# One step later for three pieces of side work, sixteen loads on another queue, and the last stores on two queues

## The chip, the cores and the metric

One NeuronCore of a Trainium2 chip runs the whole program in one launch. Its engines run side by side, each with its own instruction stream: TensorE (PE: matmuls and transposes), VectorE (DVE: elementwise work), ScalarE (ACT: copies and functions), GpSimd (POOL) and SyncE (SP: only issues DMAs). DMAs can be issued from SP, ACT and POOL; a DMA stands in the issuing engine's stream and waits there for what it needs. The metric is the device time of the program in microseconds (us), the median of the runs.

## The reference, cut to what matters

An encoder layer over x of 1024 rows and 2048 columns, in float32. `c` (one row of 2048) gives a shift, a scale and a gate for every column; the projections, the two branches and the output are large matmuls.

```python
mod = jax.nn.silu(c) @ w_ada + b_ada
shift, scale, gate = jnp.split(mod, 3, axis=-1)
h = rmsnorm(x, pre_g) * (1.0 + scale[:, None]) + shift[:, None]
q, k, v, gate_a, u, gate_p = jnp.split(h @ w_in, SPLIT_POINTS, axis=-1)
y_a = windowed_gqa(q, k, v, rel_table, sink) * jax.nn.silu(gate_a)
y_p = multiscale_pool(u, w_pool_grp, pool_scale) * jax.nn.silu(gate_p)
g_a, g_p = jnp.split(jax.nn.sigmoid(h @ w_merge + b_merge), N_BRANCHES, axis=-1)
merged = g_a * (y_a @ w_br_attn) + g_p * (y_p @ w_br_pool)
return x + gate[:, None] * rmsnorm(merged @ w_out, post_g)
```

## The kernel before

**Matmuls.** A float32 operand is split into a high and a low part that PE can multiply fast (`split`: ACT copies the high part, L96, DVE subtracts it to get the low part, L97), and a product is three matmuls: high by high, low by high, high by low. Over these lies a Strassen-like scheme (`strassen`): a block of the result comes from seven products instead of eight, named after their left operand, in the order B11, T3, T2, B21, T4, T1, B22. One product is 12 matmuls of 128x512 (6 in the first stage), into one of the PSUM banks X, V and Z. DVE and ACT add and copy the banks into one another (L114, L117, L257, L285, L302, L320); the copy of a bank is what frees it for a later product. Two of these generators overlap, so that the last product of one block (B22) runs after the first two of the next. The weights (`raw`, 512 KB a load) come from HBM through four buffers, are added to one another by DVE for the T products, and are split as above.

**Side work.** All that isn't a product hangs on these products. `run` goes through the seven, and after those that `every` lists it takes one step from a queue `side`:

```python
            if side and i in every:
                side.popleft()()
```

So a step's place in the list sets the place of its matmuls in PE's stream, and roughly that of its loads, ACT and DVE instructions. A scheduler then sets the order on every engine from program order and dependences; what is wrapped in `keep` stays in program order. Every engine works strictly through its order.

**The stages, and the side work that matters here.**

The ramp (to about 110 us) turns x, forms the columns of shift and scale for eight groups j of 256 columns and runs the first products. `late_sums` lists for its 13 side steps which parts of groups 2 and 3 they carry. A group's last part (`columns`) transposes the partial sums `acc` on PE into PM (L480), reduces them on DVE (L482) and adds and multiplies them into `modc` (L487, L490); the tiles xT are then scaled by `modc` on ACT (L567) and DVE (L568).

The first pass goes over 20 pairs of blocks of the left half of the inputs. Its side work sums further parts of w_ada into `gacc` (L536), and its last step `gate_row` takes the sums over rows with eight matmuls GATE (L885), adds and multiplies them on DVE and stores the gate's row to HBM (pg_d, L893); `late_rows` has eight matmuls PMR on the same line.

The rest of the first pass (from about 530 us) brings the right half of x. `x_step(n)` for n = 0 to 17 loads tile n (`fetch_x`, L958, load at L961, tag xt2), scales it on ACT (L962), and on every odd n transposes the tiles n-3 and n-2 on PE (`turn_x`, L968) and copies the pieces to h on ACT (L971).

The second pass has as side work the attention, the pooling, and at its end `y_steps`, which loads the 16 tiles of y_a back from HBM (ya_d, L1245) for the branch matmuls; four `pre` steps then subtract tiles y from one another on DVE (L117, tags y and tf). The same function loads y_p (yp_d) later.

At the end `out_pair` forms the output block by block. For the last two row tiles (t = 0, 1) `result` multiplies by the gate, `square` sums the squares on ACT (L1403), `scale_of` makes the row scale (L1420, L1421), and `finish_block` (L1424) multiplies by it, adds x (L1426) and stores 128x512 (L1427), for n in (0, 2, 3, 1). The block t = 1, n = 1 is the very last.

Of the kernel before, what the change touches and what calls it, by code (L numbers as in the profile page):

```python
# [15 lines left out]
AF = mybir.ActivationFunctionType  # L16
ALU = mybir.AluOpType
# [13 lines left out]
NB = S // P  # L31
# [12 lines left out]
def encoder_layer(ctx: ExitStack, tc: tile.TileContext, x, c, table, w_ada, b_ada, pre_g,  # L44
# [15 lines left out]
    nc = tc.nc  # L60
# [16 lines left out]
    def uid(s):  # L77
        cnt[0] += 1
        return f"{s}_{cnt[0]}"
# [11 lines left out]
    def keep(ins):  # L91

        tc.keep_in_program_order(ins)
# [25 lines left out]
    load = nc.sync.dma_start  # L119
    store = nc.sync.dma_start  # L120
# [9 lines left out]
    rstd = const.tile([P, NB], F32, name="rstd")  # L130
# [9 lines left out]
    ya_d = dram.tile([NH * P, S], F32, name="ya_d")  # L140
# [16 lines left out]
    def pre_op(j, h1, h2, tmp, pin=lambda ins: None):  # L157

        pin(sub(h1[j][1], h1[j][1], h1[j][0]))
        t2 = tmp()  # L160
        pin(sub(t2, h2[j][1], h1[j][1]))
        return t2
# [198 lines left out]
    held = ExitStack()  # L361
# [4 lines left out]
    for r0, src in ((0, c[0]), (16, b_ada[0, 0:D]), (32, b_ada[0, D:2 * D]),  # L366
                    (48, pre_g[0]), (64, b_merge[0]), (96, pool_scale[0])):
        n = src.shape[0] // P
# [133 lines left out]
    def modulation(j, tile_of, pin=False, apart=False):  # L502

        st_ = {}

        def step(q, between=None):
            if q == 0:
                st_["pv"] = bank("at", "GEMV")
            pv = st_["pv"]
            for kc in range(4 * q, 4 * q + 4):  # L510
                g = kc % 4 * 32
                ins = nc.tensor.matmul(pv[g:g + 32, :], scz[:, kc, :], tile_of(kc), start=kc < 4,
                                       stop=kc >= 12, tile_position=(0, g))
                if pin:
                    tc.keep_in_program_order(ins)
            if q == 3:
                acc = xa2.tile([P, 4, P], F32, tag="acc", name=uid("acc"), bufs=2)
                tc.keep_in_program_order(
                    nc.scalar.activation(acc, pv.rearrange("p (g n) -> p g n", g=4), AF.Copy))
                if between:  # L520
                    between()
                st_["acc"] = acc
                if not apart:
                    columns()

        def columns():
            mod_columns(j, sum_columns(st_["acc"]))

        return [partial(step, q) for q in range(4)] + [columns]
# [134 lines left out]

    group2 = modulation(2, ada[2].__getitem__, True, True)
    group3 = modulation(3, ada3.__getitem__, True, True)
    late_sums = {0: group2[:1], 4: group2[1:4], 5: group2[4:], 10: group3[:4], 11: group3[4:]}
    side = deque((lambda n=n: [step() for step in late_sums.get(n, ())]) for n in range(13))
    for s in range(2):
        for si in range(4 * s, 4 * s + 4):  # L670
# [249 lines left out]
    def unit_step(n):  # L920
        m = n - AHEAD
        if m in then:
            then[m]()
        if m >= 0:
            units[m][1]()
        if n < len(units):
            units[n][0]()

    side = deque(lambda n=n: unit_step(n) for n in range(len(units) + AHEAD))
    side.append(gate_row)  # L930
    EASY = ((0, 2, 4, 6), (1, 3, 5))
    n1 = 20
    sums = deque(weight_sums(j, h_) for h_ in range(2) for j in range(KT // 2))
# [24 lines left out]
    def fetch_x(si, q):  # L958
        xt = xin.tile([P, 512], F32, tag="xt2", name=uid("xt"))
        c0 = 1024 + q * 512  # L960
        load(xt, x[si * P:(si + 1) * P, c0:c0 + 512])  # L961
        nc.scalar.activation(xt, xt, AF.Copy, scale=rstd[:, si:si + 1])  # L962
        return xt

    def turn_x(si, q, xt):
        pt = bank("sc")
        for j in range(4):
            nc.tensor.transpose(pt[:, j * P:(j + 1) * P], xt[:, j * P:(j + 1) * P], ident)  # L968
        for j in range(4):
            dst = h[8 + q * 4 + j][si // 4][:, (si % 4) * P:(si % 4 + 1) * P]  # L970
            nc.scalar.activation(dst, pt[:, j * P:(j + 1) * P], AF.Copy)  # L971

    held = {}

    def x_step(n):
        if n < 2 * NB:
            held[n] = fetch_x(n // 2, n % 2)
        if n >= 3 and n % 2:
            for q in range(2):
                turn_x((n - 3) // 2, q, held.pop(n - 3 + q))  # L980

    side = deque(lambda n=n: x_step(n) for n in range(2 * NB + 2))
# [17 lines left out]
    side = deque()  # L1000
# [12 lines left out]
    with pool("attn") as ap:  # L1013
# [116 lines left out]
        def step(u, e):  # L1130
            nu = len(UNITS)
            if e == 0 and 0 <= u - LAG_V < nu:
                values(u - LAG_V)
            if e == 1 and u % 16 in (1, 3) and u < nu:
                turn_v(u % 16 // 2)
            if e == 1 and 0 <= u - LAG_T < nu:
                turn(u - LAG_T, 0)
                turn(u - LAG_T, 1)
            if u < nu:
                if u % 16 == 0 and e == 0:  # L1140
                    take_k(UNITS[u][0] * 2 // GQA)
                if u % 4 == 0:
                    split_q(e)
                scores(u, e)
            if e == 1:
                if opened:
                    gated(*opened.pop())
                if u % 4 == 3 and u + 1 < nu:
                    fetch_q(u + 1)
                c_ = u - LAG_V + 1  # L1150
                if (c_ + 1) % 16 == 0 and c_ + 1 < nu:
                    fetch_v(UNITS[c_ + 1][0] * 2 // GQA)
                if 0 <= c_ < nu:
                    if c_ % 4 == 0:
                        fetch_gate(c_)
# [83 lines left out]
    ysrc = ExitStack()  # L1239
    sp = ysrc.enter_context(pool("ysrc"))  # L1240

    def y_steps(yd, store_to):
        def get(k, s):
            t = sp.tile([P, 512], F32, tag="y", name=uid("y"), bufs=16)
            load(t, yd[k * P:(k + 1) * P, s * 512:(s + 1) * 512])  # L1245
            h1, h2, _ = store_to
            (h1 if k < 4 else h2).setdefault(k % 4, []).append(t)

        def pre(j):
            h1, h2, t2 = store_to  # L1250
            t2[j] = pre_op(j, h1, h2, lambda: sp.tile([P, 512], F32, tag="tf", name=uid("tf"), bufs=4), keep)

        return [lambda k=k, s=s: get(k, s) for k in (0, 4, 1, 5, 2, 6, 3, 7) for s in range(2)] + \
            [lambda j=j: pre(j) for j in range(4)]

    ys = [({}, {}, {}), ({}, {}, {})]
    side.extend(y_steps(ya_d, ys[0]))
    while side:
        next_pair(range(7))
    while pidx[0] < PAIRS:  # L1260
# [129 lines left out]
    def out_mm(pb, op, name, j, t, w, first, last):  # L1390
        ts_ = slice(t * P, (t + 1) * P)
        hi, lo = (o_[:, j % 2, ts_] for o_ in op[name][j // 2])
        nc.tensor.matmul(pb, hi, w[0], start=first, stop=False, skip_group_check=True)  # L1393
        nc.tensor.matmul(pb, lo, w[0], start=False, stop=False, skip_group_check=True)  # L1394
        nc.tensor.matmul(pb, hi, w[1], start=False, stop=last, skip_group_check=True)  # L1395

    xrow, held = {}, {}

    def rows_of(T, n):
        return out[T * P:(T + 1) * P, n * 512:(n + 1) * 512]  # L1400
# [18 lines left out]
    def scale_of(T, s_):  # L1419
        nc.scalar.activation(s_[:, 1:2], ssq[:, T, 1:2], AF.Sqrt, bias=s_[:, 0:1], scale=1.0 / D)  # L1420
        nc.vector.reciprocal(s_[:, 2:3], s_[:, 1:2])  # L1421
        return s_[:, 2:3]

    def finish_block(T, n, scale, store=store):  # L1424
        r = held.pop((T, n))
        keep(nc.vector.scalar_tensor_tensor(r, r, scale, xrow.pop((T, n)), op0=ALU.mult, op1=ALU.add))  # L1426
        store(rows_of(T, n), r)  # L1427

    def fetch_x_block(T, n, tile_of):
        xrow[T, n] = tile_of("xr")  # L1430
# [17 lines left out]
    def out_pair(half, i, op, between, after=None):  # L1448
# [51 lines left out]
        def result(blk, t, src, dst):  # L1500

            T, nh = half * 4 + (int(blk[1]) - 1) * 2 + t, int(blk[0]) - 1
            n = 2 * nh + i
            square(src, T, n)
            nc.vector.tensor_tensor(dst, src, g[nh], ALU.mult)
            if stays:
                held[T, n] = dst
            else:
                nc.gpsimd.dma_start(o_d[T * P:(T + 1) * P, n * 512:(n + 1) * 512], dst)
# [37 lines left out]
        for t in range(2):  # L1547
            for j, w in enumerate(last_weights):
                out_mm(bz[t], op, "B22", j, t, w, False, j == len(last_weights) - 1)
            result("12", t, bz[t], c12[t])  # L1550
            scale = scale_of(6 + t, rest[t])
            for n in (0, 2, 3, 1):
                finish_block(6 + t, n, scale)

    nextm, nextt2 = [], {}
    scales = {}
    side = deque()
# [79 lines left out]
    def third_block():  # L1637
        assert not side
        for T in (4, 5):
            scale = row_scale(T)  # L1640
            for b in range(4):
                finish_block(T, b, scale)

    out_pair(0, 0, ops[0], between_00)
    out_pair(0, 1, ops[0], between_01)
    out_pair(1, 0, ops[1], between_10)
    out_pair(1, 1, ops[1], between_11, third_block)

# [37 lines left out]
```

## Time and profile before

| what | before |
|---|---|
| runs | 2106.34, 2106.81, 2109.77 us; median 2106.81 |
| the profiled execution | 2109.9 us; its span 2107.8 us |
| PE busy | 2076.6 us (99%), 9511 matmuls |
| DVE, ACT, POOL busy | 1539.0 (73%), 1106.5 (52%), 25.5 us (1%) |
| chain that ended last | PE 90%, DMA 5%, DVE 3%, ACT 1% |
| DMA | 468.18 MB, mean 222 GB/s; SP's queue 66.6% of the 16 engines' span |

The span is the profile's time from the first to the last instruction. In a timeline a row is: start, duration, engine, line, operation, output<-inputs, shape, how many merged (x4), and in brackets how long the engine had been idle and what ended that. SPq is a DMA that SP issues; its duration is that of the issue. In the list of waits a row gives the waiting engine and line, the one waited for, and then total, times and longest.

### The profile page before, as it was taken

The numbers are of one execution on the slowest core, as the hardware profiler recorded it, in microseconds if no ns is written. First come the engines' busy times: TensorE is split into PE (matmuls) and PEld (weight loads), VectorE is DVE, ScalarE is ACT, GpSimd is POOL, SyncE is SP. The second block draws the span as 40 slices with busy tenths as digits, with TensorE's granted clock in tenths as the row PEclk, the third lists the DMA queues.
The fourth block names the chain that finished last, engine by engine and source line by source line (L and its number), as shares of the span: only waits on it lengthen the run. The fifth ranks groups of instructions, "written<-read, shape, count | busy, mean of one in ns | idle before, by whom it ended". The sixth has DMA issues, their size and how long they took to land.

```text
span 2107.8 us, 28866 instructions
## 1 busy us (share of the span) xinstructions
PE 2076.6 (99%) x9511; PEld 1707.8 (81%) x9511; DVE 1539.0 (73%) x2769; ACT 1106.5 (52%) x2105; POOL 25.5 (1%) x103
## 2 busy tenths in 40 slices
PE   6999999999999999999999999999999999999998
PEld 4688888888788888888888888888788788888886
DVE  5886777777547766677777688856857977889667
ACT  4754444444464635566665443333645644767555
POOL 0000000000000000000000000000000000000000
PEclk9999999999999999999999999999999999999999
DMA  9888688887666455454554577665745566686997
GB/s 323 293 271 273 222 271 285 269 286 241 205 220 212 137 184 188 160 173 160 183 164 154 163 243 221 218 212 192 250 158 173 175 196 200 217 314 206 292 330 251
DMA packets 303273, 468.18 MB, mean 222 GB/s; under 512 B 23939, under 2 KB 144875, under 8 KB 303124
## 3 DMA queue, kind: packets, MB, share of 16 engines
q1 hardware_dynamic: 299328, 457.79, 66.6%
q0 software_dynamic: 2336, 6.33, 0.8%
q10 hardware_dynamic: 1460, 2.22, 0.3%
q8 instruction: 74, 1.21, 0.2%
q14 instruction: 75, 0.61, 0.1%
HBM read 341.45 MB, written 126.90 MB: 222 GB/s over the span
## 4 chain that ended last, share of the span: by engine, by line
PE 90%; DMA 5%; DVE 3%; ACT 1%; issue 1%; SPq 0%; DVEq 0%; ACTq 0%
PE Z L247 30%; PE V L247 20%; PE X L247 20%; PE Z L1393 2%; PE Z L1395 2%; PE Z L1394 2%; DMA ada<-in_w_ada_dram 2%; PE X L1395 1%; PE X L1393 1%; PE X L1394 1%; PE V L1395 1%; PE V L1394 1%; PE V L1393 1%; PE PT L1103 1%; DMA xt<-in_x_dram 1%; DMA raw<-in_w_merge_dram 1%
## 5 line engine op out<-in xcount | busy, mean ns | idle before, releaser
L96 ACT ACTIVATE whi<-raw 128x512 fp32r<-128x512 f32 (+1 forms) x532 | 321.5, 606 | 510.7 <-PE Z L247 256.1
L97 DVE TENSOR_TENSOR wlo<-raw,whi 128x512 fp32r<-128x512 f32 (+1 forms) x532 | 346.9, 657 | 164.1 <-PE Z L247 122.3
L97 DVE TENSOR_TENSOR wlo<-wr,whi 128x512 fp32r<-128x512 f32 x224 | 150.5, 689 | 51.4 <-ACT whi L96 48.3
L96 ACT ACTIVATE whi<-wr 128x512 fp32r<-128x512 f32 x224 | 138.1, 629 | 87.9 <-DVE wlo L97 28.0
L114 DVE TENSOR_TENSOR raw<-raw,raw 128x512 f32<-128x512 f32 x79 | 54.5, 690 | 83.9 <-DMA raw<-in_w_merge_dram 61.7
L247 PE MATMUL X<-B11h,whi 128*128 128x512 f32 x334 | 90.8, 390 | 1.4 <-ACT c L320 1.4
L247 PE MATMUL V<-T3h,whi 128*128 128x512 f32 x334 | 90.8, 391 | 1.1 <-DVE u L114 1.1
L96 ACT ACTIVATE whi<-ws 128x512 fp32r<-128x512 f32 (+1 forms) x88 | 53.7, 610 | 72.2 <-PE X L247 65.7
L247 PE MATMUL Z<-B22h,whi 128*128 128x512 f32 x334 | 91.0, 392 | 0.0
L247 PE MATMUL Z<-T1h,whi 128*128 128x512 f32 x334 | 90.9, 390 | 0.0
L247 PE MATMUL X<-B21h,whi 128*128 128x512 f32 x334 | 90.7, 391 | 0.0
L247 PE MATMUL V<-T4l,whi 128*128 128x512 f32 x334 | 90.6, 390 | 0.1
L247 PE MATMUL V<-T4h,whi 128*128 128x512 f32 x334 | 90.6, 391 | 0.0
L247 PE MATMUL Z<-T2h,whi 128*128 128x512 f32 x334 | 90.3, 390 | 0.3 <-ACT whi L96 0.2
L247 PE MATMUL Z<-T2h,wlo 128*128 128x512 f32 x334 | 90.3, 390 | 0.3 <-DVE wlo L97 0.3
L247 PE MATMUL X<-B11l,whi 128*128 128x512 f32 x334 | 90.4, 390 | 0.0
L247 PE MATMUL Z<-T1l,whi 128*128 128x512 f32 x334 | 90.4, 390 | 0.0
L247 PE MATMUL Z<-B22l,whi 128*128 128x512 f32 x334 | 90.3, 390 | 0.0
L247 PE MATMUL Z<-B22h,wlo 128*128 128x512 f32 x334 | 90.2, 390 | 0.1
L247 PE MATMUL V<-T3l,whi 128*128 128x512 f32 x334 | 90.2, 390 | 0.0
L247 PE MATMUL X<-B21l,whi 128*128 128x512 f32 x334 | 90.2, 390 | 0.0
L247 PE MATMUL Z<-T1h,wlo 128*128 128x512 f32 x334 | 90.2, 390 | 0.0
(363 smaller groups left out, 4811.6 us busy)
## 6 DMA issues: line engine op xcount, KB each, us to landing
part<-part_d SPq DMA_DIRECT2D x136, 256.0 KB, 4.8
ada<-in_w_ada_dram SPq DMA_DIRECT2D x128, 256.0 KB, 5.6
raw<-in_w_merge_dram SPq DMA_DIRECT2D x64, 512.0 KB, 5.5
raw<-in_w_in_dram SPq DMA_DIRECT2D x62, 512.0 KB, 4.1
wr<-ws_dS SPq DMA_DIRECT2D x60, 512.0 KB, 5.3
wr<-in_w_out_dram SPq DMA_DIRECT2D x48, 512.0 KB, 5.1
proj_d<-part SPq DMA_DIRECT2D x68, 256.0 KB, 2.2
sw<-in_w_out_dram SPq DMA_DIRECT2D x64, 256.0 KB, 5.8
```

The lines of the kernel that those rows point to most:

```text
L96: ins = (nc.scalar.activation(hi, src, AF.Copy), nc.vector.tensor_tensor(lo, src, f32(hi), ALU.subtract))
L97: nc.vector.tensor_tensor(lo, src, f32(hi), ALU.subtract))
L114: return (eng or nc.vector).tensor_tensor(o, a, b, ALU.add)
L247: nc.tensor.matmul(ps, w_[:, i], op[mov][j][m_], start=fresh and i == 0 and n == 0, stop=i == nj - 1 and n == 2, skip_group_check=True)
L1103: nc.tensor.transpose(pt[:, i * P:(i + 1) * P], p[:, i * P:(i + 1) * P], ident)
L1393: nc.tensor.matmul(pb, hi, w[0], start=first, stop=False, skip_group_check=True)
L1394: nc.tensor.matmul(pb, lo, w[0], start=False, stop=False, skip_group_check=True)
L1395: nc.tensor.matmul(pb, hi, w[1], start=False, stop=last, skip_group_check=True)
```

## The change

Five edits. (1) The last part of group 3 of the modulation is taken at side step 12 of the ramp instead of 11. (2) An empty step stands ahead of `gate_row`, which so comes one step later. (3) The ACT scaling of an x tile moves from `fetch_x` to `x_step`, one step after the tile's load, and is kept in program order. (4) The 16 loads of y_a are issued by POOL instead of SP. (5) In the last two row tiles the blocks n = 2, 3 are stored from ACT's queue instead of SP's, and the very last block is computed and stored in two halves of 256 columns, the first from SP, the second from ACT.

```diff
-    late_sums = {0: group2[:1], 4: group2[1:4], 5: group2[4:], 10: group3[:4], 11: group3[4:]}
+    late_sums = {0: group2[:1], 4: group2[1:4], 5: group2[4:], 10: group3[:4], 12: group3[4:]}
...
-    side.append(gate_row)
+    side.extend((lambda: None, gate_row))
...
         load(xt, x[si * P:(si + 1) * P, c0:c0 + 512])
-        nc.scalar.activation(xt, xt, AF.Copy, scale=rstd[:, si:si + 1])
         return xt
...
             held[n] = fetch_x(n // 2, n % 2)
+        if 0 < n <= 2 * NB:
+            keep(nc.scalar.activation(held[n - 1], held[n - 1], AF.Copy, scale=rstd[:, (n - 1) // 2:(n - 1) // 2 + 1]))
...
-    def y_steps(yd, store_to):
+    def y_steps(yd, store_to, load=load):
...
-    side.extend(y_steps(ya_d, ys[0]))
+    side.extend(y_steps(ya_d, ys[0], nc.gpsimd.dma_start))
...
-    def finish_block(T, n, scale, store=store):
-        r = held.pop((T, n))
-        keep(nc.vector.scalar_tensor_tensor(r, r, scale, xrow.pop((T, n)), op0=ALU.mult, op1=ALU.add))
-        store(rows_of(T, n), r)
+    def finish_block(T, n, scale, store=store, halves=False):
+        r, xr = held.pop((T, n)), xrow.pop((T, n))
+        for k, queue in enumerate((nc.sync.dma_start, nc.scalar.dma_start) if halves else (store,)):
+            c_ = slice(k * 256, (k + 1) * 256) if halves else slice(0, 512)
+            keep(nc.vector.scalar_tensor_tensor(r[:, c_], r[:, c_], scale, xr[:, c_], op0=ALU.mult, op1=ALU.add))
+            queue(rows_of(T, n)[:, c_], r[:, c_])
...
-                finish_block(6 + t, n, scale)
+                finish_block(6 + t, n, scale, (store, nc.scalar.dma_start)[n // 2], halves=t and n == 1)
```

What moves, at three places. PE in the ramp around edit 1, before and then after. PM is the transposes of group 3's sums, V T4 and Z T1 are products of six matmuls:

```order
L247 MATMUL X_937<-B21h_317,wlo_1012 128x512
L247 MATMUL X_937<-B21h_377,wlo_1012 128x512
L480 MATMUL PM_1025<-ident,acc_1009 128x128 x4
L247 MATMUL V_939<-T4h_321,whi_1034 128x512
L247 MATMUL V_939<-T4h_381,whi_1034 128x512
L247 MATMUL V_939<-T4l_322,whi_1034 128x512
L247 MATMUL V_939<-T4l_382,whi_1034 128x512
```
```order
L247 MATMUL V_939<-T4l_322,whi_1025 128x512
L247 MATMUL V_939<-T4l_382,whi_1025 128x512
L247 MATMUL V_939<-T4h_321,wlo_1026 128x512
L247 MATMUL V_939<-T4h_381,wlo_1026 128x512
L480 MATMUL PM_1037<-ident,acc_1009 128x128 x4
L247 MATMUL Z_938<-T1h_325,whi_1046 128x512
```

The four transposes have moved behind the product T4. In the same way GATE (edit 2) has moved behind two products of 12 matmuls, Z B22 and Z T2, and stands ahead of X B21.

ACT around edit 3, at about 593 to 608 us of the profile before. xt_1161 to xt_1204 are the x tiles 8 to 13 in the order of their loads (1161, 1167, 1179, 1187, 1195, 1204); c_1176 and c_1192 are the copies that free a Z and an X bank. Before, the scalings of 1161 and 1167 stand some 17 rows further up; first the rows around 1179 and 1187, then those around c_1192:

```order
L257 ACTIVATE p7_1173_5626<-V_1164_5565 128x512
L962 ACTIVATE xt_1179_5655<-xt_1179_5655,rstd_80 128x512
L567 ACTIVATE h10_0_5183<-h10_0_5183,modc_79 128x512
L962 ACTIVATE xt_1187_5686<-xt_1187_5686,rstd_80 128x512
L96 ACTIVATE whi_1196_5748<-raw_1144_5454 128x512
L320 ACTIVATE c_1176_5644<-Z_1125_5360 128x512
```
```order
L971 ACTIVATE h15_1_5194<-b_1189_5698 128x128
L567 ACTIVATE h14_0_5191<-h14_0_5191,modc_79 128x512
L962 ACTIVATE xt_1195_5745<-xt_1195_5745,rstd_80 128x512
L320 ACTIVATE c_1192_5723<-X_1162_5563 128x512
L962 ACTIVATE xt_1204_5788<-xt_1204_5788,rstd_80 128x512
```

After, at the same two places:

```order
L257 ACTIVATE p7_1173_5625<-V_1164_5564 128x512
L567 ACTIVATE h10_0_5183<-h10_0_5183,modc_79 128x512
L978 ACTIVATE xt_1187_5685<-xt_1187_5685,rstd_80 128x512
L96 ACTIVATE whi_1196_5747<-raw_1144_5453 128x512
L320 ACTIVATE c_1176_5643<-Z_1125_5359 128x512
L978 ACTIVATE xt_1167_5586<-xt_1167_5586,rstd_80 128x512
```
```order
L970 ACTIVATE h15_1_5194<-b_1189_5697 128x128
L96 ACTIVATE whi_1208_5810<-ws_1207_5808 128x512
L567 ACTIVATE h13_0_5189<-h13_0_5189,modc_79 128x512
L320 ACTIVATE c_1192_5722<-X_1162_5562 128x512
L567 ACTIVATE h14_0_5191<-h14_0_5191,modc_79 128x512
```

No scaling stands around c_1192 any more, and the scaling of tile 1167 now comes behind that of tile 1187, which was loaded later.

SP around edit 4, at about 1404 to 1420 us. raw_13644 and raw_13804 are weight loads, part and proj_d are loads and stores of partial results, before and then after:

```order
L325 DMA proj_d<-u_2683_13416 128x512
L1245 DMA y_13640<-ya_d 128x512
L219 DMA part_13484<-part_d 128x512
L219 DMA part_13486<-part_d 128x512
L325 DMA proj_d<-p_2676_13360 128x512
L219 DMA part_13488<-part_d 128x512
L219 DMA part_13490<-part_d 128x512
L197 DMA raw_13644<-in_w_merge_dram 128x4x256
L1245 DMA y_13674<-ya_d 128x512
L1245 DMA y_13696<-ya_d 128x512
```
```order
L325 DMA proj_d<-u_2683_13416 128x512
L197 DMA raw_13644<-in_w_merge_dram 128x4x256
L219 DMA part_13484<-part_d 128x512
L219 DMA part_13486<-part_d 128x512
L325 DMA proj_d<-p_2676_13360 128x512
L219 DMA part_13488<-part_d 128x512
L219 DMA part_13490<-part_d 128x512
L325 DMA proj_d<-part_13320 128x512
L197 DMA raw_13804<-in_w_merge_dram 128x4x256
```

The y loads are gone from SP, and the weight load raw_13644 stands ahead of the part loads instead of behind them.

## The prediction

> **What bounds the kernel now.** I read the page first, for its busy times.
>
> ```profile
> PE 2076.6 (99%) x9511; PEld 1707.8 (81%) x9511; DVE 1539.0 (73%) x2769; ACT 1106.5 (52%) x2105; POOL 25.5 (1%) x103
> ```
>
> TensorE (PE) is busy for 2076.6 of 2107.8 us. No matmul is added or removed, so only the 31 us in which PE stands still can change. Next came the list of PE's waits, which says where those stand. These three rows are the ones that the change aims at:
>
> ```profile
> PE X L247 <- ACT c L320: 1.4, 1, 1.4
> ...
> PE V L247 <- DVE u L114: 1.1, 1, 1.1
> PE PM L480 <- ACT acc L519: 1.0, 1, 1.0
> ```
>
> Each is a single wait of a little over 1 us (total, times, longest). A fourth, before GATE, lies inside a merged row of the timeline and is shown below. The list's larger waits stand in the first tens of microseconds, at lines that the change leaves alone. So the ceiling is small: four single waits and the tail behind the last matmul. The timeline around each, one engine at a time, gives the price.
>
> **Edit 1, PM one side step later.** PE, then ACT, then DVE around 90 us:
>
> ```profile
> 89.86 0.62 PE L247 MATMUL X<-B21h,wlo 128*128 128x512 f32 x2
> 91.52 0.66 PE L480 MATMUL PM<-ident,acc 128*128 128x128 f32 x4 [1.04 <-ACT acc L519]
> ...
> 97.50 0.62 PE L247 MATMUL Z<-B22h,whi 128*128 128x512 f32 x2
> ...
> 98.86 0.39 PE L247 MATMUL Z<-T2h,whi 128*128 128x512 f32 x1
> ```
> ```profile
> 94.48 1.52 ACT L567 ACTIVATE xT<-xT,modc 128x512 f32<-128x512 f32 x2 [0.86 <-DVE modc L490]
> ...
> 97.52 0.58 ACT L285 ACTIVATE Z<-X 128x512 f32<-128x512 f32 x1
> ```
> ```profile
> 94.95 0.68 DVE L114 TENSOR_TENSOR u<-V,u 128x512 f32<-128x512 f32 x1
> 95.55 0.41 DVE L97 TENSOR_TENSOR wlo<-raw,whi 128x256 fp32r<-128x256 f32 x1
> ```
>
> Six matmuls go from 97.50 to 98.86, so one takes 0.227 us. The two at 89.86 are through at 90.31, and PM starts at 91.52: 1.21 us are lost, 0.17 more than the 1.04 in brackets (the restart). With the six matmuls of T4 (1.36 us) moved ahead, PM is due at 91.67, after acc has come, and the wait goes. What is late next: PE's following products are then due 1.2 us earlier, but modc is not. PM itself runs 0.15 later than before, and the addition at 94.95 (L114, 0.68 us), which stood behind modc on DVE, now stands ahead of the reduction, so modc comes not just ahead of 94.48 but at about 95.2. ACT's scaling by modc (L567) waits for it, with the copies of u and of Z queued behind. From the first scaling to the Z copy it was 3.04 us (94.48 to 97.52); the new order has two splits fewer in between, so I estimate 2.3: the copy starts at about 97.5 and ends at 98.1. T2, which needs it, would be due at 98.86 - 1.21 = 97.65. I take 0.7 us of the 1.21 back as a new wait there or just ahead of it: gain 0.5, with ends of 1.2 (DVE's order costs nothing) and a loss of 0.3 (modc a whole microsecond later yet).
>
> **Edit 2, the gate row one side step later.**
>
> ```profile
> 529.17 2.11 PE L885 MATMUL GATE<-gacc,onez 128*32 128x512 f32 x8
> ```
> ```profile
> 528.89 1.28 DVE L536 SCALAR_TENSOR_TENSOR gacc<-gada,sc,gacc 128x1024 f32<-128x1024 f32 x1
> ```
> ```profile
> 353.37 1.06 PE L885 MATMUL PMR<-acc,onez 128*32 128x512 f32 x8
> ```
>
> The same eight matmuls of the same shape took 1.06 us where their operands lay ready, and 2.11 here, since gacc was written until 530.17: 1.05 us lost. Moved behind two products of 12 matmuls (24 x 0.227 = 5.4 us) they start at about 534.6, 4.4 us after gacc. The weights of the two products that come forward are split ahead of them on ACT and DVE without waiting for gacc. The stores to pg_d go later by as much; they are read only in the output stage. Gain 1.05, and at least 0.8 if the first of those products should wait a little.
>
> **Edit 3, the scaling of x one step after its load.** ACT and PE around 600 us:
>
> ```profile
> 597.06 0.72 ACT L962 ACTIVATE xt<-xt,rstd 128x512 f32<-128x512 f32 x1 [3.51 <-DMA xt<-in_x_dram]
> ...
> 606.97 0.72 ACT L962 ACTIVATE xt<-xt,rstd 128x512 f32<-128x512 f32 x1 [1.72 <-DMA xt<-in_x_dram]
> 607.60 0.58 ACT L320 ACTIVATE c<-X 128x512 f32<-128x512 f32 x1
> ```
> ```profile
> 597.64 1.03 PE L968 MATMUL b<-ident,xt 128*128 128x128 f32 x8
> ...
> 608.23 0.96 PE L247 MATMUL X<-B11h,whi 128*128 128x512 f32 x3 [1.36 <-ACT c L320]
> ```
>
> The copy that frees PSUM bank X (c, L320) stands in ACT's order behind a scaling that waits for its load; PE loses 1.36 us, 1.5 with the restart as above. In the new order no scaling stands right before that copy, and it runs some 3 us earlier: that wait goes. But the scheduler has also put tile xt_1187 ahead of xt_1167 (the order above shows it). The transposes at 597.64 read xt_1161 and xt_1167; before, both had been scaled long ago. Now ACT, which fell idle at 597.06 - 3.51 = 593.55 and has one more modulation to do first (to about 594.3), waits for xt_1187, whose load was issued after the one that ended the wait at 597.06 and landed at about 598.4 at the latest; only then does it run a split, the copy c_1176 and the scaling of xt_1167. A scaling holds ACT for 0.63 us (606.97 to 607.60), the others a little less, so xt_1167 is done some 2.3 us after the landing. The load is issued behind a store that waits for DVE, which has less to wait for on ACT now; I put the landing 1 to 2 us earlier, at 596.2. Then xt_1167 is scaled at 598.5 and its four transposes, due at 598.1 or so, start some 0.5 us late. Net gain 1.5 - 0.6 = 0.9. Ends: 1.5 (the load lands by 595.8), and a loss of 1.2 (it lands at 598.4 as before: 600.7 against 598.1 is 2.6 to 2.7 of new wait).
>
> **Edit 4, the y loads through POOL's queue.** SP, DVE and PE around 1410 us:
>
> ```profile
> 1396.12 1.86 SPq L1245 DMA_DIRECT2D y<-ya_d  x3
> ...
> 1403.89 0.32 SPq L325 DMA_DIRECT2D proj_d<-u  x1
> ...
> 1408.85 0.48 SPq L197 DMA_DIRECT2D raw<-in_w_merge_dram  x1
> ...
> 1418.20 0.32 SPq L325 DMA_DIRECT2D proj_d<-part  x1
> ...
> 1420.07 0.38 SPq L197 DMA_DIRECT2D raw<-in_w_merge_dram  x1
> ```
> ```profile
> 1416.87 0.69 DVE L114 TENSOR_TENSOR raw<-raw,raw 128x512 f32<-128x512 f32 x1 [4.26 <-DMA raw<-in_w_merge_dram]
> ...
> 1427.30 0.69 DVE L117 TENSOR_TENSOR ws<-raw 128x512 f32<-128x512 f32 x1 [5.52 <-DMA raw<-in_w_merge_dram]
> ```
> ```profile
> 1428.74 1.17 PE L247 MATMUL V<-T3h,whi 128*128 128x512 f32 x4 [1.13 <-DVE u L114]
> ```
>
> The first raw load is issued at 1408.85 and lands at 1416.87, 8.0 us later, among y loads; DVE waits in order, the store at 1418.20 waits for DVE, and the second raw load stands behind that store and three more y loads: issued at 1420.07, there at 1427.2. DVE's addition that frees bank V stands behind it, and PE waits 1.13 us (1.3 with the restart). Without y loads on SP, the first raw load stands ahead of the four part loads, right behind the store of 1403.89, and can go at about 1404.3; it lands 6 to 8 us later, by 1412.3. The store follows DVE as it does now, 1.3 us after the landing, at about 1413.6, the second raw load at 1414, and with its own 7.1 us it lands at about 1421. PE wants V at about 1427.4, and DVE has two operations of 0.6 to 0.7 to do for it, so the load is needed by 1426: some 5 us to spare, and the wait goes whole, 1.3. On POOL nothing is queued behind these loads until the next section; who waits for them is DVE's subtraction at 1454.59:
>
> ```profile
> 1454.59 0.69 DVE L117 TENSOR_TENSOR y<-y,y 128x512 f32<-128x512 f32 x1
> ...
> 1466.14 0.69 DVE L117 TENSOR_TENSOR tf<-y,y 128x512 f32<-128x512 f32 x1
> ```
> ```profile
> 1850.55 0.54 POOL L1509 DMA_DIRECT2D o_d<-u  x1 [10.12 <-DVE u L1505]
> 1851.75 0.54 POOL L1509 DMA_DIRECT2D o_d<-u  x1 [0.66 <-DVE u L1505]
> ```
> ```profile
> out_dram<-mo POOLq DMA_DIRECT2D x8, 256.0 KB, 6.4
> ```
>
> A POOL issue of this size holds POOL 0.54 us, and stores of it landed after 6.4 us in the median. With all in flight the 16 loads are there 16 x 0.54 + 6.4 = 15 us after the first, with half of them in flight at a time some 30: by 1426, well before 1454. Ends: gain 1.3, or nothing if the y packets slow the raw loads as much as now.
>
> **Edit 5, the last stores.**
>
> ```profile
> 2100.02 0.58 ACT L1403 ACTIVATE junk<-Z 128x512 f32<-128x512 f32 x1 [4.36 <-PE Z L1395]
> ```
> ```profile
> 2103.53 0.74 DVE L1426 SCALAR_TENSOR_TENSOR c<-c,st,xr 128x512 f32<-128x512 f32 x1
> ...
> 2104.31 0.33 SPq L1427 DMA_DIRECT2D out_dram<-c  x1
> ```
> ```profile
> 2104.00:2105.00 1.00, 0.00 (x0) 0.00 (x0) 0.28 (x1) 0.00 (x0) 0.00 (x0) 0.82 1.07 369
> ```
>
> The square at 2100.02 still starts right after the last matmul: the ACT stores of the row tile before have long had their data. The last block becomes two pieces of 256 columns; 256 columns cost DVE 0.41 against 0.68 for 512 in the rows of edit 1, so together they take some 0.14 longer; the last issue comes at 2104.4 while the first half leaves 0.3 earlier, and the last transfer is half as large. In the fullest microsecond of the tail the DMA engines were busy throughout (share 1.07, 369 GB/s), at which 128 KB are 0.36 us. I take a gain of 0.2, with ends of 0.5 and a loss of 0.2 (two issues and two completions instead of one). The Trainium skill, "Trainium Kernel Development and Optimization", Key Constraints, says that DMAs from SP, ACT and POOL run on the same 16 engines, so that several issuing engines save only issue time: by it the edit would give 0 here and the sum would be 0.2 smaller; the row of full DMA engines bears it out, the halved last transfer speaks the other way.
>
> **Sum.** 0.5 + 1.05 + 0.9 + 1.3 + 0.2 = 3.95 us. The profiled execution, 2109.9 us (span 2107.8), would become 2105.95. It lies 3.1 us above the median of the three runs, 2106.81, so a median of 2102.9 is expected.
>
> **The rivals.** *All waits go, and nothing is late next.* 1.2 + 1.05 + 1.5 + 1.3 + 0.3 = 5.35: 2101.5. For it: each wait is single, and PE has no other near. Against it: the order of ACT in edit 3 and DVE's in edit 1 put something new ahead of what PE needs.
>
> *ACT's new queue costs more than the old one.* If the load of xt_1187 lands at 598.4 as before, edit 3 loses 1.2: 0.5 + 1.05 - 1.2 + 1.3 + 0.2 = 1.85, or 2105.0. For it: the 3.51 us wait at 597.06 shows that these loads do come in late. Against it: the store that stands ahead of the load on SP waits for work behind ACT's old wait.
>
> *Slower: POOL's loads go one at a time.* Place: the 16 y loads. If each must land before the next is sent, at 6.4 us each, they need 102 us from 1396 and the last is there at 1498.5, while DVE, in order, wants the last ones at 1466.14: about 32 us late, everything behind them on DVE waits, and PE with it: 2102.9 + 32 = 2135. It decides from a spacing of (1466 - 1396)/15 = 4.7 us. Against it: the two stores at 1850.55 and 1851.75 were issued 1.2 us apart, far less than one landing. The Trainium skill, "SBUF — State Buffer", section on SBUF's two separate sides, warns of this direction: a DMA issued from GpSimd needs its descriptors written by GpSimd, which some VectorE operations lock out. This trace has POOL issues of 0.54 us beside a VectorE that is 73% busy, which speaks against a lockout of microseconds.
>
> *The change does not do what it says in one place* (a wait comes back behind the next product, or a later gap grows by what was won): 2 us of gain are left, 2104.8.
>
> **How the numbers follow.** Forecast 0.44, at 2102.9 with about 1.2 us to either side; all waits gone 0.24; ACT's new queue 0.16; a gain lost later 0.10; POOL one at a time 0.06. About 0.2% (4.2 us, a median below 2102.6 or above 2111.0) is what a measurement of this kernel can tell from no change. The forecast lies just inside it: I put 0.18 of its 0.44 beyond. So faster is 0.18 + 0.24 = 0.42, slower 0.06, the same 0.52. The range takes in the full gain with 0.7 us for how executions differ, 2100.8, and on the other side ACT's new queue with edits 1 and 4 at their poor ends (0.5 + 1.3 less gain), 2106.8; outside it stay the serial loads and the outer ends, under 2 in 10.
>
> **What would show it right or wrong.** In the new profile the four waits (PM on acc, GATE on gacc, X on c, V on u) should be gone from PE's list; a wait of about 0.5 us on an ACT copy or scaling near 97 us and one on xt (L978) near 598 us should be new. The raw loads at 1405 and 1415 should be issued ahead of where they were, y loads stand on POOL at some 0.54 us each, and the end should come 7.3 to 7.8 us after the last square starts. It is wrong if a wait of more than 2 us stands at the transposes (L970's readers), if DVE waits for y at 1450 to 1470, or if the span's end comes more than 7.8 us after the last square (2100.02 to 2107.8 before).

## The result, and the profile after

The changed kernel took 2103.89 us (median of 11 runs, 2102.23 to 2106.19), the kernel before, beside it, 2107.36 (11 runs, 2105.41 to 2112.21): a ratio of 0.9983, 95% interval 0.9975 to 0.9991. That is 3.6 us less by the ratio, 1.9 to 5.3 by its interval. The forecast was 2102.9 within 2100.8 to 2106.8.

The page of the profile after and then PE's list of waits (waiting line, the one waited for, total, times, longest):

```profile
span 2100.4 us, 28893 instructions
...
PE 2072.7 (99%) x9511; PEld 1708.7 (81%) x9511; DVE 1541.0 (73%) x2770; ACT 1107.9 (53%) x2105; POOL 33.9 (2%) x119
```
```profile
PE PB L696 <- ACT B11h L567: 1.2, 2, 0.7
PE Z L247 <- DVE wlo L97: 0.4, 1, 0.4
...
PE b L967 <- ACT xt L978: 0.2, 1, 0.2
```

Of the four waits aimed at, PM, X and V are not in it (GATE's, inside a merged row, was in neither list), and of the two new ones that the prediction expected, one is: 0.2 us of the transposes on the scaling of x. The two spans differ by 7.4 us, twice what the medians do: that pair of traces flatters the change, and it took more traces to see which part lasts.

The places of the prediction in the timeline after. PE in the ramp and at the gate:

```profile
89.48 0.62 PE L247 MATMUL X<-B21h,wlo 128*128 128x512 f32 x2
...
91.30 0.60 PE L480 MATMUL PM<-ident,acc 128*128 128x128 f32 x4
...
97.26 0.73 PE L247 MATMUL Z<-T2h,whi 128*128 128x512 f32 x2
```
```profile
533.12 1.06 PE L885 MATMUL GATE<-gacc,onez 128*32 128x512 f32 x8
```

ACT and PE around 600 us:

```profile
593.55 0.72 ACT L978 ACTIVATE xt<-xt,rstd 128x512 f32<-128x512 f32 x1 [1.67 <-DMA xt<-in_x_dram]
...
601.30 0.65 ACT L320 ACTIVATE c<-X 128x512 f32<-128x512 f32 x1
```
```profile
595.94 0.66 PE L967 MATMUL b<-ident,xt 128*128 128x128 f32 x4 [0.25 <-ACT xt L978]
```

SP, then POOL, which now issues the y loads, and then DVE around 1400 us:

```profile
1400.40 0.38 SPq L197 DMA_DIRECT2D raw<-in_w_merge_dram  x1
...
1414.69 0.38 SPq L197 DMA_DIRECT2D raw<-in_w_merge_dram  x1
```
```profile
1391.37 3.70 POOL L1246 DMA_DIRECT2D y<-ya_d  x7 [0.58 <-issue]
```
```profile
1410.24 0.69 DVE L114 TENSOR_TENSOR raw<-raw,raw 128x512 f32<-128x512 f32 x1 [7.07 <-DMA raw<-in_w_merge_dram]
...
1419.26 0.69 DVE L117 TENSOR_TENSOR ws<-raw 128x512 f32<-128x512 f32 x1 [1.59 <-DMA raw<-in_w_merge_dram]
```

The second weight load is there at 1419.2, 8.0 us earlier than before, in a program that was 4.1 us ahead at that place; DVE is through with the addition that frees bank V at 1420.6, 2.8 us before PE wants it.

### The profile page after: what moved, and what is told of

The parts are those of the page before. It is cut to its first block, busy times and chain, and to the rows that moved or that the text cites. A ratio compares the mean times of both kernels' runs of the same rounds, so it can differ in the third digit from the quotient of the medians.

```text
span 2100.4 us, 28893 instructions
## 1 busy us (share of the span) xinstructions
PE 2072.7 (99%) x9511; PEld 1708.7 (81%) x9511; DVE 1541.0 (73%) x2770; ACT 1107.9 (53%) x2105; POOL 33.9 (2%) x119
## 3 DMA queue, kind: packets, MB, share of 16 engines
q8 instruction: 74, 1.21, 0.2%
## 4 chain that ended last, share of the span: by engine, by line
PE 94%; DMA 1%; DVE 1%; ACT 0%; issue 0%; DVEq 0%; ACTq 0%
PE Z L247 32%; PE X L247 21%; PE V L247 21%; PE Z L1394 2%; PE Z L1396 2%; PE Z L1395 2%; PE X L1395 1%; PE X L1396 1%; PE X L1394 1%; PE V L1395 1%; PE V L1394 1%; PE V L1396 1%; PE PT L1104 1%; PE PV L1115 0%; PE PV L1116 0%; PE PV L1114 0%
## 5 line engine op out<-in xcount | busy, mean ns | idle before, releaser
L247 PE MATMUL X<-B21h,wlo 128*128 128x512 f32 x334 | 90.1, 389 | 0.0
```

The source lines that it names most:

```text
L247: nc.tensor.matmul(ps, w_[:, i], op[mov][j][m_], start=fresh and i == 0 and n == 0, stop=i == nj - 1 and n == 2, skip_group_check=True)
```

## The experiments

Twelve kernels ran. Since a single wait of 1 us is half a thousandth of the time, the traces carry most of the verdicts. For each I took the starts of PE's matmuls (every trace has 9511 of them, with the same work between the numbers taken here) and the time in us between two of them around each place: numbers 330 to 480 (ramp, PM), 2300 to 2400 (GATE), 2600 to 2720 (x), 6500 to 6620 (around 1427 us) and 6850 to 6980 (1480 to 1512 us), and for the tail from the last matmul's start to the span's end.

| kernel | edits | ramp | GATE | x | 1427 | 1495 | tail | ratio (interval) |
|---|---|---|---|---|---|---|---|---|
| before | none | 31.37 | 23.20 | 26.74 | 28.59 | 31.21 | 8.20 | 1 |
| e0_before | none | 30.23 | 22.90 | 26.15 | 27.48 | 30.01 | 8.21 | 0.9999 (0.9989 to 1.0009) |
| e1_pm | 1 | 31.38 | 22.99 | 25.82 | 27.55 | 29.84 | 8.20 | 0.9996 (0.9986 to 1.0005) |
| e2_gate | 2 | 30.74 | 22.15 | 25.31 | 27.31 | 31.01 | 8.19 | 0.9997 (0.9987 to 1.0006) |
| e3_scale | 3 | 31.02 | 22.94 | 26.53 | 27.20 | 30.60 | 8.19 | 1.0004 (0.9994 to 1.0013) |
| e4_pool | 4 | 30.13 | 23.03 | 26.43 | 27.20 | 29.47 | 8.20 | 0.9991 (0.9983 to 1.0000) |
| e24 | 2, 4 | 30.13 | 22.15 | 26.01 | 27.20 | 29.47 | 8.21 | 0.9982 (0.9973 to 0.9991) |
| e13 | 1, 3 | 31.24 | 23.22 | 25.63 | 27.20 | 31.07 | 8.21 | 0.9996 (0.9987 to 1.0004) |
| after | all | 30.30 | 22.15 | 25.55 | 27.20 | 29.47 | 8.25 | 0.9983 (0.9975 to 0.9991) |
| after_again | all | 30.19 | 22.15 | 25.98 | 27.20 | 29.47 | 8.23 | 0.9986 (0.9977 to 0.9995) |
| roots | none, 2 queues | 30.13 | 23.21 | 27.75 | 27.23 | 30.75 | 8.43 | 1.0004 (0.9995 to 1.0013) |
| best_q | 2, 4, part of 5, 2 queues | 30.13 | 22.15 | 28.47 | 27.20 | 29.47 | 8.48 | 0.9992 (0.9983 to 1.0001) |
| after_roots | all, 2 queues | 30.13 | 22.15 | 26.99 | 27.20 | 29.47 | 8.55 | 1.0005 (0.9996 to 1.0014) |
| best_pool_add | 2, 4, 2 queues | 30.13 | 22.15 | 27.30 | 27.20 | 29.47 | 11.31 | 0.9995 (0.9987 to 1.0004) |

("2 queues": the ramp's stores and the loads of x moved to POOL, as shown further below.)

**The kernel before, once more.** No edit.

> The kernel before, unchanged, for a second trace. Theory A (the four waits are set by the order of the instructions): PM on acc 1.0, GATE on gacc 0.9, X on c 1.4 and V on u 1.1 us stand in PE's list again, each within 0.4. Theory B (the other 2 us or so by which the two traces differ, at 1498 to 1512 above all, are scatter between executions): PE's loss there is not 1.7 again but anything from 0 to 2. Theory C (that loss belongs to y loads on SP and is cured by edit 4): 1.7 again, within 0.3.

PM's wait was not there at all, V on u was absent from the list, and of X on c this was left:

```profile
PE X L247 <- ACT c L320: 0.8, 1, 0.8
```

Theory A fell for three of the four waits: between these two executions of the same program they differ by 0.6 to 1.1 us. Only GATE's is there in every trace without edit 2. At 1495 it was 30.01 instead of 31.21: what is lost there scatters too, as theory B said, and C fell with its 1.7. Both values are still above the changed kernel's 29.47.

**Edits 1, 2 and 3 alone.**

```diff
-    late_sums = {..., 11: group3[4:]}
+    late_sums = {..., 12: group3[4:]}
```

> Edit 1 alone. Theory A: PM's wait on acc goes and nothing takes its place, PE is 1.2 us earlier at the first pass; GATE, X on c and V on u keep their waits. My forecast's own step: 0.5 net, with a wait of 0.7 on the copy of Z ahead of Z T2. In the time 1.2 us is 0.06%, below what three rounds can tell; the trace decides.

PM's wait was gone, and PE lost 1.25 us, nearly all of it over the products that follow, the largest piece ahead of Z B22:

```profile
95.75 0.82 ACT L567 ACTIVATE xT<-xT,modc 128x512 f32<-128x512 f32 x1 [2.08 <-DVE modc L490]
96.47 0.57 ACT L302 ACTIVATE u<-Z 128x512 f32<-128x512 f32 x1
```
```profile
97.10 0.73 PE L247 MATMUL Z<-B22h,whi 128*128 128x512 f32 x2 [0.37 <-ACT u L302]
```

This is the chain that the forecast named (modc, the scaling, the copy of u), at nearly twice the price, though in the trace of the whole change it cost 0.2. Both have the same order of instructions in the ramp. What differs stands some 10 us earlier on ACT, in the kernel before as in this one:

```profile
87.00 0.60 ACT L320 ACTIVATE c<-Z 128x512 f32<-128x512 f32 x1 [2.74 <-DMA ramp_d<-c]
```

The copy c needs a tile that a store to ramp_d must first have read, and the copy that makes acc for PM (L519) stands behind c in ACT's order. Counted from the start of the products on PE whose sums become acc (GEMV, L512), c came after 0.25, 0.31, 0.61, 1.12, 1.39 and 1.74 us in the six traces with neither edit 1 nor a new queue, and the ramp lost 0, 0, 0.10, 0.61, 0.89 and 1.24. In the four with edit 1 it came after 0.75, 0.83, 1.77 and 1.91, and 0.06, 0.17, 1.11 and 1.25 were lost. So the loss is this lateness less 0.5 without edit 1 and less 0.66 with it: edit 1 is worth at most 0.16 us, and moves the wait.

```diff
-    side.append(gate_row)
+    side.extend((lambda: None, gate_row))
```

> Edit 2 alone. GATE's eight matmuls take 1.06 instead of 2.11 us, 1.05 us gained, and PM, X on c and V on u keep their waits. Rival: with PE not yet 1.2 us earlier, the products brought forward wait for their split weights (0.2 to 0.5 us) and 0.6 to 0.8 is left. Time: 0.05%, too little to be seen.

22.15 in this trace and in every later one with edit 2, against 22.90 to 23.22 without: 0.9 us (mean 23.05) that doesn't scatter. The rival had no wait to show for it.

```diff
-        nc.scalar.activation(xt, xt, AF.Copy, scale=rstd[:, si:si + 1])
...
+        if 0 < n <= 2 * NB:
+            keep(nc.scalar.activation(held[n - 1], held[n - 1], AF.Copy, scale=...))
```

> Edit 3 alone. Theory A: X on c (1.4) is gone, and a wait of 0.2 to 0.6 us of the transposes on the scaling of x stands near 598 us; net gain 1.0 to 1.3. Rival (the landing of that load decides and it comes as late as in the kernel before): a wait of up to 2.6 us there, and PE loses 1.2 us net. The other three waits stay.

X on c was gone, and the transposes waited 1.24 us for the scaling of tile 1167. That one stands in ACT's order behind the scaling of 1187, which waited for its load (the first row):

```profile
596.40 0.72 ACT L978 ACTIVATE xt<-xt,rstd 128x512 f32<-128x512 f32 x1 [2.66 <-DMA xt<-in_x_dram]
```
```profile
598.79 0.66 PE L967 MATMUL b<-ident,xt 128*128 128x128 f32 x4 [1.24 <-ACT xt L978]
```

The stretch took 26.53 us; over the traces it is 26.08 on average without edit 3 (six traces, 25.31 to 26.74) and 25.92 with it (four, 25.55 to 26.53): 0.16 us, within its scatter. This formed theory D, that edits 1 and 3 trade one wait for another.

**Edit 4 alone, the pairs 2 with 4 and 1 with 3, and the change again.**

```diff
-    def y_steps(yd, store_to):
+    def y_steps(yd, store_to, load=load):
...
-    side.extend(y_steps(ya_d, ys[0]))
+    side.extend(y_steps(ya_d, ys[0], nc.gpsimd.dma_start))
```

> Edit 4 alone. Four traces without edit 4 so far lost between 0 and 1.4 us at V T3 near 1427 and between 0.2 and 1.7 us at 1495 to 1512. Theory D (edits 1 and 3 only trade one wait for another, the lasting gain is that of edits 2 and 4): PE's stretch around 1427 takes 27.2 us and the one at 1480 to 1512 at most 29.8, gain 1 to 2.4 us, ratio 0.9989 to 0.9995. Theory A (each edit gains what the first pair of traces showed at its place): 1.4 us, all of it near 1427, ratio 0.9993, and the stretch at 1480 to 1512 scatters as before.

> Edits 2 and 4 without 1, 3 and 5. Theory D: all of the change's lasting gain, 2 to 3.5 us, ratio 0.9983 to 0.9990, no slower than the whole change. Theory A: 2.5 us, 0.9988, and the whole change is 2.4 us faster than this.

> Edits 1 and 3 without 2, 4 and 5. Theory D: no gain within 0.7 us, ratio 0.9997 to 1.0003; in the trace PM's wait and X's wait on c are gone, and waits on the copy of u ahead of Z B22 near 96 us or of the transposes on the scaling of x near 598 us stand in their place. Theory A: 2.4 us, 0.9989, without new waits above 0.3 us.

> The changed kernel again, for a second trace and more runs. Theory D: ratio 0.9980 to 0.9990; the waits that edits 1 and 3 leave (u ahead of Z B22, scaling ahead of the transposes) differ from the first trace by up to 1 us, those of edits 2 and 4 stay at nothing. Theory A: none of them above 0.3 us, as in the first trace, 0.9977 to 0.9983.

Theory D held, though 0.9982 for edits 2 and 4 and 0.9996 for edits 1 and 3 each lie one ten-thousandth outside the range given. The whole change has 0.9983 and 0.9986. The ratio of edits 1 and 3 alone would leave room for theory A too (0.9989 is inside its interval). What decides is that the whole change is no faster than edits 2 and 4, 2104.46 against 2104.40 us side by side, where A asked for 2.4 us, and that the waits come back in the traces: e13's trace shows the traded wait (31.24 in the ramp; its PE waited 0.4 us on u ahead of Z B22) and after_again the other one (0.7 us at the transposes).

Edit 4 gains at two places. Around 1427 it takes away a loss that the six traces without it had at 0 to 1.39 us, 0.36 on average. At 1480 to 1512, where the forecast saw nothing, it gains 1.15: 29.47 in every trace with it, 29.84 to 31.21 without. There PE waits for splits of the branch operand on a DVE that has been busy almost without a pause for some 40 us. The same four matmuls on PE, before and then after, and the row of e13's list that names the wait:

```profile
1497.83 1.56 PE L247 MATMUL V<-T4l,whi 128*128 128x512 f32 x4
```
```profile
1492.36 1.07 PE L247 MATMUL V<-T4l,whi 128*128 128x512 f32 x4
```
```profile
PE V L247 <- DVE T4l L97: 0.5, 1, 0.5
```

DVE, before and then after, where that busy stretch begins:

```profile
1452.65 0.69 DVE L114 TENSOR_TENSOR raw<-raw,raw 128x512 f32<-128x512 f32 x1 [4.86 <-DMA raw<-in_w_merge_dram]
```
```profile
1444.72 0.69 DVE L114 TENSOR_TENSOR raw<-raw,raw 128x512 f32<-128x512 f32 x1 [3.48 <-DMA raw<-in_w_merge_dram]
```

Counted from matmul 6620 of each trace, this addition comes at 12.2 to 13.4 us in the six traces without edit 4 and at 10.2 to 10.3 in the four with it; its weight load is issued at 5.8 to 7.0 against 4.0. In the kernel before the last y load left SP 25 us ahead of that weight load: the lateness of SP's loads around 1410 is handed on from one weight load to the next, until DVE's backlog of y subtractions and splits turns it into PE's wait.

**Two late DMAs on POOL's queue.** Theory E: the waits of edits 1 and 3 hang on a store and a load that SP issues late.

```diff
-                store(block(ramp_d[0], 0)(blk), t)
+                nc.gpsimd.dma_start(block(ramp_d[0], 0)(blk), t)
...
-        load(xt, x[si * P:(si + 1) * P, c0:c0 + 512])
+        nc.gpsimd.dma_start(xt, x[si * P:(si + 1) * P, c0:c0 + 512])
```

> The kernel before with none of the five edits; instead the four stores of the plain blocks in the ramp (L701) and the 16 loads of x (L961) are issued by POOL, so that they don't stand in SP's order. Theory E (the waits that edits 1 and 3 aim at hang on one DMA each that SP issues late: a ramp store that frees a tile for ACT's copy c, and an x load; reordering the instructions around them changes little): PM's wait on acc and X's wait on c are gone, PE's stretch from the fourth group of the modulation to the end of that block takes 30.1 to 30.2 us (30.1 to 31.4 before), the one around 600 us 25.3 to 25.6 (25.3 to 26.7 before); gain about 0.5 + 0.7 us. Rival (the order of ACT and DVE is what binds): waits of 0.5 us or more remain in both. GATE and the stretches at 1427 and 1495 keep their losses. Ratio 0.9992 to 0.9998.

For the ramp it held. The four stores, before and then here:

```profile
L701 SPq DMA_DIRECT2D ramp_d<-c x4: 320/329/343, 81.3 to 83.5; - x4
```
```profile
L701 POOL DMA_DIRECT2D ramp_d<-c x4: 539/539/577, 67.7 to 70.0; - x4
```

They go 13.6 us earlier (first and last start in the row), ACT's copy c waits for nothing, and the ramp takes 30.13 in all four kernels with this queue, with edit 1 or without. For x it fell: 26.99 to 28.47, worse than every trace with x on SP (26.74 at most). The ratio of 1.0004 missed the range of theory E.

```profile
590.79 1.08 POOL L961 DMA_DIRECT2D xt<-in_x_dram  x2 [7.98 <-PE b L968]
```
```profile
599.47 0.72 ACT L962 ACTIVATE xt<-xt,rstd 128x512 f32<-128x512 f32 x1 [3.85 <-DMA xt<-in_x_dram]
```
```profile
PE Z L247 <- ACT u L257: 1.5, 1, 1.5
```

POOL waits for the transposes that free the tile, issues at 590.79, and ACT has the tile only at 599.4, 8.6 us later. The same tile issued by SP 1.3 us later (counted from the same matmul) in the kernel before took 6.0 us.

**Edits 2 and 4 on top of the two queues, and two looks at the tail.**

```diff
-                finish_block(6 + t, n, scale)
+                finish_block(6 + t, n, scale, (store, nc.scalar.dma_start)[n // 2])
```

> Edits 2 and 4, the POOL issues of the run before, and of edit 5 the split of the last stores between two queues, without halves. Theory E: all four waits and the loss at 1495 are gone, 3.5 to 4.5 us, ratio 0.9978 to 0.9984. Tail: if the last issue and its landing set the end and not the bytes or the queue, the end comes 8.19 to 8.21 us after the last matmul starts, as in the kernel before; if sharing two queues helps, 8.1 or less; if the second queue costs something, 8.25.

> The changed kernel with the two POOL issues added, so edits 1 and 3 stand where the late DMAs are gone. Theory E: nothing more to gain from them, within 0.5 us of the run before; tail 8.23 to 8.25. Rival (edit 1 or 3 helps for a reason of its own): faster than that run by 1 us or more at 90 to 98 or 590 to 608 us.

In the kernel that follows, block n = 2 of the very last row tile leaves DVE:

```diff
+        if T == 7 and n == 2:
+            nc.scalar.activation(r, r, AF.Copy, scale=scale)
+            nc.gpsimd.tensor_tensor(r, r, xrow.pop((T, n)), ALU.add)
...
```

> Edits 2 and 4 and the two POOL issues, all last stores on SP; one of the last row tile's four blocks (n = 2) is scaled on ACT and added to x on POOL, which takes one of four operations of 0.66 us off DVE's chain behind the last matmul. If the last issue sets the end, the tail shortens from 8.2 to 7.5 or 7.6 us, unless POOL's addition (not seen in any trace so far, 0.6 to 2 us) becomes the last itself: then 8.0 to 9. In all 4 to 5 us less than the kernel before.

None beats the change, nor e24: what x loses on POOL, and 0.2 us and more in the tail (8.48 and 8.55 where at most 8.25 was expected), eat the ramp's gain. In the trace of after_roots, edits 1 and 3 add nothing but at x, where 26.99 is the least of the four. Its time missed the expectation: a median of 2108.76 us against best_q's 2105.36 side by side, not within 0.5. The traces do not show where that is lost, since the one of after_roots is of an execution of 2106.59 us and the one of best_q of 2108.07; it stays open. POOL's addition made the tail 3.1 us longer, beyond the 8 to 9 allowed for:

```profile
2096.03 1.73 POOL L1428 TENSOR_TENSOR mo<-mo,xr 128x512 f32<-128x512 f32 x1 [56.81 <-ACT mo L1427]
2096.55 1.75 DVE L1430 SCALAR_TENSOR_TENSOR c<-c,st,xr 128x512 f32<-128x512 f32 x1
```

It took 1.73 us, and DVE's last operation, 0.75 elsewhere, took 1.75 beside it.

## Why the prediction was right, point by point

**The total was right and its parts were not.** From the means of the table the change gains 0.16 (edit 1 at equal lateness) + 0.90 + 0.16 + 0.36 + 1.15 - 0.04 = 2.7 us by its places, inside the intervals of both measurements of it (1.9 to 5.3, and 1.1 to 4.8). The remaining 0.9 of the 3.6 is not placed: the head and the attention scatter by more than that. That the total came out so near is in part luck. Edits 1 and 3 were taken at 1.4 against 0.3, and a gain of 1.15 at 1495, which no term held, made up for it. Nor was the trace that gave the prices an average one: its execution took 3.1 us more than the median of three, and in the ramp, at x, at 1427 and at 1495 its stretch is the longest of the six traces without the edit. Taking its waits off the median counts some that the median does not have.

**Edit 1**, forecast 0.5, is worth 0.16 at most. The step of a new wait behind modc was right in kind; in the first trace after it was absent, because DVE came to its addition ahead of the reduction at 93.01 already; in e1_pm, where c was 1.08 us later, it came to it at 94.34. The step that failed is that PM's 1.21 is a price of the order: it was one draw of a store's landing.

**Edit 2**, forecast 1.05, is worth 0.90; the mechanism and the cover were right.

**Edit 3**, forecast 0.9 with ends of 1.5 and -1.2, is worth 0.16 on average. The new order of xt_1187 ahead of xt_1167 did what was worked out, 0.25 to 1.24 us of new wait against the 0.6 forecast. The mis-sized term was the old wait, taken at 1.5 from one trace; the others without edit 3 had between nothing and 1.1. The rival on ACT's new queue came about by half in e3_scale.

**Edit 4**, forecast 1.3, is worth 1.5, of which 0.36 stands where the forecast put it. The step that failed is that its effect ends when the wait at 1427 is gone. The first weight load left as worked out, at 1404.5 on the clock of the kernel before (4.1 us are added), but took 9.75 us instead of 6 to 8: with edit 4 it takes 8.9 to 9.8 us in every trace of the table, 6.9 to 8.0 without. So the second left at 1418.8 and not at 1414, and 2.8 us were to spare instead of 5. The slower rival didn't come: POOL issued the seven loads of the row above 0.53 us apart, with several in flight, and the last of the 16 landed at 1409.8. DVE waits for no y tile. Of a lockout by VectorE, which the Trainium skill, "SBUF — State Buffer", section on SBUF's two separate sides, warns of, these loads show nothing. That page also says of two operations that want the shared ports that the one that starts first keeps them and the other stands still. best_pool_add has one such pair and agrees in the main: DVE's operation of 0.75, which started 0.52 us after POOL's, ran 1.75 us and ended 0.54 after POOL's.

**Edit 5**, forecast 0.2, costs 0.04, and the sign of being wrong that the prediction named for it came: the end is 7.82 us after the last square starts, 7.77 before. The step that failed is that a last transfer half as large ends earlier. The DMA engines in the last microseconds, before and then after (stretch, busy times, clock, DMA share, GB/s):

```profile
2105.00:2106.00 1.00, 0.00 (x0) 0.00 (x0) 0.00 (x0) 0.00 (x0) 0.00 (x0) 0.50 0.98 356
```
```profile
2096.00:2097.00 1.00, 0.00 (x0) 0.00 (x0) 0.98 (x3) 0.00 (x0) 0.00 (x0) 1.00 1.01 369
2097.00:2098.00 1.00, 0.00 (x0) 0.00 (x0) 0.00 (x0) 0.00 (x0) 0.00 (x0) 0.57 1.05 353
```

Four stores are 1.05 MB, and at some 350 GB/s that is 3.0 us from the first packet, 3.55 us after the last matmul's start, to the last at 6.58 before, 6.60 in best_q with two queues and 6.63 after with halves as well. The engines had no gap in that time, so the bytes set the end. The rule that the prediction weighed against the edit (the Trainium skill, "Trainium Kernel Development and Optimization", Key Constraints: several issuing engines save issue time alone) gave 0, and was nearer than the 0.2 that I took.

## What to carry to other kernels

A wait read from one trace is one draw. Before an instruction is moved out of a wait's way, follow the wait back to its root: where that is a DMA's landing, the reordered program waits for the same DMA elsewhere, and the price of the wait is its mean over several traces. What pays is to take transfers that nobody waits for yet out of the queue ahead of those that somebody does; that gain can surface tens of microseconds later, where an engine's backlog meets PE.

## What was not expected

POOL's queue is no free road: beside SP's own loads and stores, x tiles of 256 KB of the right half took up to 9.9 us from POOL (best_q) against 6.7 at most from SP (e3_scale). Behind the last data packet the span ran on for 1.62 us in the kernels before and after, but 1.9 in best_q and after_roots, which issue 20 more DMAs from POOL, and 3.7 in best_pool_add; what fills that time the traces don't show, and it stays open.
